# The inverse's identity written by GpSimd, sigmoids as tanh, and copies and scalings moved to ScalarE in the mixing stage of a hybrid decoder step

## The chip, the cores and the metric

The kernel runs on one core of a Trainium2 chip. A core has a matrix engine (TensorE, PE in the profile, its weight loads shown as PEld), VectorE (DVE), ScalarE (ACT), GpSimd (POOL) and SyncE (SP), which here only issues DMAs. The engines run side by side, each through a queue of its own in a fixed order, and wait for one another by semaphores. The metric is the time on the device of one execution, in microseconds (us).

## The reference

One layer of a decoder on 256 prompt tokens and 8 sampled tokens, all in fp32, with a width of 2048:

```python
x = x + 0.5 * swiglu(rmsnorm(x, n1), f1g, f1u, f1d)     # width 5504
proj = rmsnorm(x, nm) @ w_in
o_att  = sliding-window attention over q, k, v (16 heads of 64, window 128, sinks, relative bias)
o_rwkv = rwkv_time_mix(the other columns of proj)        # 16 heads of 64
x = x + concat(o_att, o_rwkv) @ w_out
x = x + 0.5 * swiglu(rmsnorm(x, n2), f2g, f2u, f2d)      # then a final rmsnorm
```

The part that the change touches is the second half of the mixing. The softmax of the attention is `exp(s - m) / denom`. The time mixing goes by these lines, where `a` is the rate and `g` the output gate:

```python
w = -softplus(-(w0 + tanh(wl) @ w2)) - 0.5;  logw = -exp(w)
a = sigmoid(a0 + al @ a2)
g = sigmoid(gl) @ g2
kk = k * k_k;  kk = kk / max(norm(kk), 1e-12)            # per head
k = k * (1.0 + (a - 1.0) * k_a)
S = S * exp(logw) + (S @ -kk) (kk * a)^T + v k^T;  y = S @ r   # token by token
```

## The kernel before

**Data and gemms.** The 264 tokens (256 + 8) are the free axis of every large product; the 2048 features lie in 16 tiles of 128 partitions. Each fp32 product is made of three products of a split, `hi*hi`, `hi*lo` and `lo*hi`. A weight block of four tiles (`chunk`, line 116) is loaded by SyncE's queue into a raw buffer, rounded to its high part by ScalarE (line 123), and the low part is the difference, on VectorE (the call on line 124, shown under line 58, the helper `tt`). Six raw buffers and four pairs of high and low parts go round. Twelve matmuls of 128x264 belong to one block (`gemm`, line 127).

**Stages.** First feed-forward, mixing (`mixing_body`, line 332), second feed-forward. In the mixing the input product is made tile by tile (`win`, line 365): two tiles for the low-rank inputs and the gate (lines 819 to 822), then three tiles for each of eight pairs of heads, then keys and values, then eight query tiles. Its result feeds small tasks, written as coroutines, which are moved on by one step after every weight block; `pause` puts a number of such steps between two parts of a task (`DWAIT`, `PW`). So the matmuls of a task stand among those of the gemms.

**The tasks.** `prep` (from line 392), one for each pair of heads: two small products give the decay and the rate, two sigmoids on ScalarE (lines 401, 402), the key's norm on VectorE (line 412), two exponentials of the running decay (lines 416 to 418), the rate's steps (lines 423 to 427), the decayed keys (`KR`, line 431), and copies of the eight sampled columns to `XD` by GpSimd (line 436). A pair's scores within a chunk of 64 tokens go to memory (`sa`).

`chain` (from line 516), one for each batch of two pairs, four batches: it inverts the unit triangular matrices of the delta rule. The 32x32 blocks are read back spread over partitions, as `X` and `Y` (shown as `Xt`; lines 528, 529); 30 steps of a substitution run on VectorE (lines 535 to 542). The result, which lacks the ones on its diagonal, is stored to memory (`sb`, line 544) by four transfers and read again into `TT` (line 549) in the layout of the matrix engine. VectorE then adds the identity to four blocks (lines 552 to 556), two transposes give `TN` (line 559), and products follow: TN's (line 566) copied to `zs` by ScalarE (571), `zs` with `TT` copied by ScalarE into `TT` (580), `TT` with `KR`. The last gives `W`, copied by ScalarE (594), and `uv`, copied by VectorE in two halves per pair (596). Then `PT` (610), `N` (626), three steps of the state, the output `y` (649) and a group norm (`gnorm`).

`softmax` (line 701) is called by each of eight `attend` tasks on four tiles, two of 128x256 and two of 128x128, and by `dec_attend` on one: four exponentials with their sums on ScalarE, a reciprocal and four scalings on VectorE. The maximum comes with the scores (`mxv`, line 732).

**Output product.** It goes in three passes over the heads (`PASS`): pairs 0 to 3 of the time mixing, pairs 4 to 7, and the attention. Ahead of each pass its inputs are split on ScalarE (line 858) and on VectorE and GpSimd in turn (line 859).

**Order.** The order of the program is made at build time by a list scheduler which knows the engines and estimates durations; the weight blocks have high priority and a few instructions are pinned. The code therefore gives the order only up to that scheduler: an edit of one task can move the instructions of others in all queues. Between the two programs here, the first 6566 and the last 6512 matrix instructions of 15622 stand in the same order; what differs lies in the mixing.

Of the kernel before, what the change touches and what calls it, by code (L numbers as in the profile page):

```python
# [9 lines left out]
AF = mybir.ActivationFunctionType  # L10
ALU = mybir.AluOpType
AX = mybir.AxisListType

P = 128
NP = 256
NB = 8
T = NP + NB
# [7 lines left out]
HALF = (slice(0, 64), slice(64, 128))  # L25
# [17 lines left out]
VMU, VKK, VKA, VA0, VRK, VLW, VLB, VSK, VSD = 64, 90, 98, 106, 114, 122, 130, 138, 154  # L43
# [4 lines left out]
def body(tc, I, O):  # L48
    nc = tc.nc
    V, A, G, TE, SP = nc.vector, nc.scalar, nc.gpsimd, nc.tensor, nc.sync  # L50
# [6 lines left out]
    def tt(e, out, a, b, op):  # L57
        return e.tensor_tensor(out=out, in0=a, in1=b, op=op)  # L58

    def stt(out, a, s, b, op0, op1):  # L60
        return V.scalar_tensor_tensor(out=out, in0=a, scalar=s, in1=b, op0=op0, op1=op1)  # L61

    def ts(e, out, a, s1, op0, s2=None, op1=None):
        k = {} if op1 is None else dict(op1=op1)
        e.tensor_scalar(out=out, in0=a, scalar1=s1, scalar2=s2, op0=op0, **k)

    def act(out, in_, f, **k):
        return A.activation(out=out, in_=in_, func=f, **k)  # L68

    def bc(ap, shape):  # L70
        return ap.broadcast_to(list(shape))
# [19 lines left out]
    def pause(n):  # L91
        for _ in range(n):
            yield

    with ExitStack() as ctx:
# [7 lines left out]
        def slot(shape=(P, T), dt=F32, tag="s"):  # L103
            return sp.tile(list(shape), dt, tag=tag, bufs={"s": NS, "o": NO, "y": NY}[tag], name=uid(tag))

        def tmp(shape=(P, T), dt=F32):
            pool, n = cur[0]
            return pool.tile(list(shape), dt, tag="t", bufs=n, name=uid("t"))
# [4 lines left out]
        def mp():  # L113
            return pp.tile([P, 512], F32, tag="m", bufs=NM, name=uid("m"))
# [28 lines left out]
        vec = cp.tile([P, NVEC], F32, name="vec")  # L143
# [13 lines left out]
        def vc(i):  # L157
            return vec[:, i:i + 1]
# [168 lines left out]
        def mixing(n2, n3, XD):  # L327
            with tc.tile_pool(name="mx", bufs=1) as mx:
                cur[0] = (mx, NT)
                return mixing_body(mx, n2, n3, XD)  # L330

        def mixing_body(mx, n2, n3, XD):
            def fix(shape, name):
                return mx.tile(list(shape), F32, name=name)

            def ring(shape, tag, bufs):
                return mx.tile(list(shape), F32, tag=tag, bufs=bufs, name=uid(tag))
# [6 lines left out]
            ident, bo, cm = C[:, CID:CID + P], C[:, CBO:CBO + P], C[:, CCM:CCM + P]  # L344
# [7 lines left out]
            for pj in PJ:  # L352
                G.memset(pj[:, 0:1], 0.0)
            nmu = fix((P, NSH), "nmu")
            mu = vec[:, VMU:VMU + NSH]
            ts(V, nmu, mu, -1.0, ALU.mult, 1.0, ALU.add)
            tt(V, ss, ss, bc(mu.unsqueeze(2), (P, NSH, NB)), ALU.mult)
# [15 lines left out]
            def shifted(t, d):  # L373
                ps = win(t)
                pj = PJ[t % 3]
                with tc.high_priority():
                    tt(V, pj[:, 1:1 + T], ps[:, :T], rs, ALU.mult)
                G.tensor_copy(shc[:, t, :], pj[:, NP:NP + NB + 1])
                act(d[:, :NP], pj[:, 0:NP], AF.Copy, scale=vc(VMU + t))
                A.copy(d[:, NP:], ss[:, t, :])  # L380
                stt(d, pj[:, 1:1 + T], nmu[:, t:t + 1], d, ALU.mult, ALU.add)
                return d

            la, sgl = fix((P, T), "la"), fix((P, T), "sgl")
# [4 lines left out]
            def c4(x):  # L389
                return x[:, :NP].rearrange("p (c t) -> p c t", c=4)  # L390

            def prep(p, bt, k, xrr, xk, xv):
                lw = load(I["lw"][p], (P, 256))
                zp = mp()
# [3 lines left out]
                ap = mp()  # L398
                mm(ap[:, :T], lw[:, P:2 * P], la)
                sg, a = tmp(), tmp()  # L400
                act(sg, zp[:, :T], AF.Sigmoid)
                act(a, ap[:, :T], AF.Sigmoid, bias=vc(VA0 + p))
                kk, b = tmp(), tmp()
                act(kk, xk, AF.Copy, scale=vc(VKK + p))
                act(b, kk, AF.Square)
# [8 lines left out]
                W, Wi = tmp((P, 4, 65)), tmp((P, 4, 64))  # L414
# [5 lines left out]
                yield from pause(PW[1])  # L420
                rk = tmp((P, T + 2 * NB))
                stt(b, b, 1e24, kk, ALU.min, ALU.mult)
                tt(V, b, b, a, ALU.mult)
                ts(V, a, a, 1.0, ALU.subtract, vc(VKA + p), ALU.mult)
                kx = a
                stt(kx, a, 1.0, xk, ALU.add, ALU.mult)
                stt(rk[:, :T], xrr, vc(VRK + p), kx, ALU.mult, ALU.mult)
                yield
                BK, KR = ring((P, 4, 3, 64), "bk", 2), ring((P, 3, 4, 64), "kr", NKR)
                bt.KR[k] = KR  # L430
                stt(KR[:, 0], c4(kk), -1.0, W[:, :, 0:64], ALU.mult, ALU.mult)
                tt(V, KR[:, 1], c4(xrr), W[:, :, 1:65], ALU.mult)
                s4 = (P, 4, 2, 64)
                tt(V, BK[:, :, 0:3:2, :], bc(c4(b).unsqueeze(2), s4), bc(Wi.unsqueeze(2), s4), ALU.mult)
                tt(V, BK[:, :, 1, :], c4(kx), Wi, ALU.mult)
                for i, src in ((6, kk), (2, b), (3, xv), (4, kx), (5, xrr)):
                    G.tensor_copy(XD[:, i, p, :], src[:, NP:T])
                dq = rk[:, T:].rearrange("p (s b) -> p s b", s=2)
                tt(G, XD[:, 7, p, :], XD[:, 1, p, :], XD[:, 5, p, :], ALU.mult)
# [31 lines left out]
                for h in range(2):  # L471
# [3 lines left out]
                    for blk in range(2):  # L475
                        x = blk * 32
# [39 lines left out]
            def chain(bt):  # L516
                n = bt.n
                while bt.left:
                    yield
                nr = n * 16  # L520
                ng = P // nr
                if ng == 3:
                    ng = 2
                nj = 32 // ng
                X = ring((ng * nr, 32, 32), "X", 1)
                Y = ring((ng * nr, nj, 32), "Xt", 1)
# [4 lines left out]
                TT = ring((P, n * 4, 64), "TT", NTT)  # L531
# [3 lines left out]
                for s in range(1, 31):  # L535
                    m, w = -(-s // ng), 31 - s
                    t = ring((ng * nr, m, w), "st", 2)
# [3 lines left out]
                    if s % NSTEP == 0:  # L541
                        yield
                for g in range(ng):
                    SP.dma_start(scr2[bt.i].rearrange("r (j g t) -> g r j t", g=ng, t=32)[g], Y[g * nr:(g + 1) * nr])  # L544
                yield from pause(1)
                for h in range(2):
                    for blk in range(2):
                        x = h * 64 + blk * 32
                        SP.dma_start(TT[x:x + 32, :, blk * 32:blk * 32 + 32],
                                     scr2[bt.i].rearrange("(h b m) (s t) -> h b s m t", h=2, b=2, s=32)[h, blk])  # L550
                yield from pause(DWAIT[bt.i])
                for h in range(2):
                    for blk in range(2):
                        x = h * 64 + blk * 32
                        v = TT[x:x + 32, :, blk * 32:blk * 32 + 32]
                        tt(V, v, v, bc(ident[x:x + 32, x:x + 32].unsqueeze(1), (32, n * 4, 32)), ALU.add)
                TN = ring((P, n * 4, 32), "TN", 1)
                for h in range(2):
                    V.transpose(TN[h * 64:h * 64 + 32], TT[h * 64:h * 64 + 32, :, 0:32])
# [2 lines left out]
                for k in range(n):  # L562
                    for c in range(4):
                        for h in range(2):
                            j = k * 4 + c
# [17 lines left out]
                uv = bt.UV  # L583
                W, PT = ring((P, n, 3, 64), "W", 1), ring((P, n, 3, 64), "PT", 1)
# [7 lines left out]
                for k in range(n):  # L592
                    v = wus[k].rearrange("p (c t) -> p c t", c=4)
                    A.copy(W[:, k], v[:, 1:4, 0:64])
                    for h in range(2):
                        V.tensor_copy(uv[HALF[h], :, k, HALF[h]], v[HALF[h], :, 64:128])
                yield
                pbs = [mp() for _ in range(n)]
                for k in range(n):
                    for c in range(1, 4):  # L600
                        x = (c - 1) * P
# [6 lines left out]
                for k in range(n):  # L608
                    v = pbs[k][:, :384].rearrange("p (c t) -> p c t", c=3)
# [3 lines left out]
                for k in range(n):  # L613
                    for c in range(4):
                        x = (k * 4 + c) * 64
# [3 lines left out]
                for k in range(n):  # L619
                    for c in range(4):  # L620
                        x = (k * 4 + c) * 64
# [8 lines left out]
                for c in range(1, 4):  # L630
# [5 lines left out]
                    for k in range(n):  # L636
                        for h in range(2):
                            r = HALF[h]
                            x = (k * 4 + c) * 64
# [20 lines left out]
                for k in range(n):  # L660
                    p, o = bt.p0 + k, Ys[k]
# [39 lines left out]
            def softmax(s, mxv, sinks, n):  # L701
                nm, sm, es = (ring((P, 4), "st" + x, 6) for x in "abc")
                ts(V, nm[:, :n], mxv[:, :n], -1.0, ALU.mult)
                for j in range(n):
                    act(s[j], s[j], AF.Exp, bias=nm[:, j:j + 1], accum_out=sm[:, j:j + 1])
                w = n // len(sinks)
                for h, x in enumerate(sinks):
                    act(es[:, h * w:(h + 1) * w], nm[:, h * w:(h + 1) * w], AF.Exp, bias=x)
                tt(V, sm[:, :n], sm[:, :n], es[:, :n], ALU.add)
                V.reciprocal(sm[:, :n], sm[:, :n])  # L710
                for j in range(n):
                    ts(V, s[j], s[j], sm[:, j:j + 1], ALU.mult)

            def attend(t, q):
                p = t // 4
# [12 lines left out]
                for h, sps in enumerate(spp):  # L728
                    s1, s0 = sc[h]
                    head = (2 * p + h) * 4 + t % 4  # L730
                    for s, a, b, j in ((s1, sps[:, 0:256], bs[h], 0), (s0, sps[:, 256:384], bs[h][:, P:256], 1)):
                        V.tensor_tensor_reduce(out=s, in0=a, in1=b, op0=ALU.add, op1=ALU.max, scale=1.0,  # L732
                                               scalar=vc(VSK + head), accum_out=mxv[:, 2 * h + j:2 * h + j + 1])
                softmax([x for y in sc for x in y], mxv, [vc(VSK + (2 * p + h) * 4 + t % 4) for h in range(2)], 4)
                yield
                yield from pause(PW[4])
# [82 lines left out]
            shifted(0, la)  # L819
            act(tw[0:64, :], la[0:64, :], AF.Tanh)  # L820
            shifted(1, sgl)
            act(sgl, sgl, AF.Sigmoid)
            bat, att, bts = [], [], []
            for kind, i in SEQ:
                if kind == "b":
                    bt = newbatch(i)
                    for k in range(BATCH[i]):
                        p = bt.p0 + k
                        x = [shifted(2 + 3 * p + j, tmp()) for j in range(3)]
# [5 lines left out]
                elif kind == "kv":  # L835
                    w, p = i // 2, i % 2
                    ps = win(LKV + i)
                    x = slot()
# [86 lines left out]
        with tc.tile_pool(name="dx", bufs=1) as dx:  # L925
            XD = dx.tile([P, 8, NPAIR, NB], F32, name="XD")
# [101 lines left out]
```

## Time and profile before

| | |
|---|---|
| time, median of 3 runs | 2034.14 us (2033.25 to 2035.09) |
| the profiled execution | 2030.2 us |
| its span in the trace | 2028.1 us |
| mean granted TensorE clock | 0.996 |
| busy: PE, DVE, ACT, POOL | 98%, 65%, 51%, 12% |

The profiled execution took 2.1 us more than its span, which runs from the first to the last instruction that the trace shows. Rows of a view name the line of the kernel, the engine, the operation and its output and inputs (`TT<-TT,C` reads the tiles TT and C and writes TT); behind the bar stand the busy time, the mean duration of one in ns, and the idle time of the engine just before such instructions with what ended it. `A <- B: 5.3, 5, 1.5` in the views of waits reads: A waited for B, 5.3 us in total, 5 times, 1.5 at the longest. In a timeline, a row starts with its start and its duration; a value in square brackets is the idle time of the engine before it. A granted clock of 1.00 is TensorE's full rate.

### The profile page before, as it was taken

The numbers are of one execution on the slowest core, as the hardware profiler recorded it, in microseconds if no ns is written. First come the engines' busy times: TensorE is split into PE (matmuls) and PEld (weight loads), VectorE is DVE, ScalarE is ACT, GpSimd is POOL, SyncE is SP. The second block draws the span as 40 slices with busy tenths as digits, with TensorE's granted clock in tenths as the row PEclk, the third lists the DMA queues.
The fourth block names the chain that finished last, engine by engine and source line by source line (L and its number), as shares of the span: only waits on it lengthen the run. The fifth ranks groups of instructions, "written<-read, shape, count | busy, mean of one in ns | idle before, by whom it ended". The sixth has DMA issues, their size and how long they took to land.

```text
span 2028.1 us, 45390 instructions
## 1 busy us (share of the span) xinstructions
PE 1994.5 (98%) x17096; PEld 1956.8 (96%) x17096; DVE 1321.9 (65%) x2623; ACT 1035.2 (51%) x2027; POOL 240.9 (12%) x337
## 2 busy tenths in 40 slices
PE   9999999999999999999999899999999999999998
PEld 9999999999999999998898789999999999999998
DVE  5865555655556577678778766775666666666665
ACT  5644444444444466665555455554444444444445
POOL 0301001010110122111100010120101101010012
PEclk9999999999999999999999899999999999999999
DMA  6565655655556566554455345465566555655654
GB/s 226 178 187 196 184 193 188 185 185 176 186 170 192 181 207 204 155 159 121 134 148 166 91 133 185 171 184 178 191 181 195 180 192 189 187 191 180 195 181 145
DMA packets 227421, 358.38 MB, mean 177 GB/s; under 512 B 42353, under 2 KB 80769, under 8 KB 227201
## 3 DMA queue, kind: packets, MB, share of 16 engines
q1 hardware_dynamic: 220752, 346.95, 55.0%
q10 hardware_dynamic: 6448, 8.53, 1.3%
q8 instruction: 134, 2.20, 0.5%
q14 instruction: 87, 0.70, 0.1%
HBM read 347.25 MB, written 10.21 MB: 176 GB/s over the span
## 4 chain that ended last, share of the span: by engine, by line
PE 93%; DVE 3%; DMA 2%; ACT 1%; issue 1%; SPq 0%; ACTq 0%; DVEq 0%
PE acc L74 84%; PE m L74 7%; DVE lo L58 1%; DMA TT<-sb 1%; DMA sb<-Xt 0%; DMA raw<-in_win 0%; DVE y L58 0%; ACT t L68 0%; DVE t L678 0%; DMA raw<-in_gu 0%; DVE Xt L58 0%; DVE st L58 0%; ACT L68 0%; SPq L544 0%; DVE t L732 0%
## 5 line engine op out<-in xcount | busy, mean ns | idle before, releaser
L58 DVE TENSOR_TENSOR lo<-raw,hi 128x512 fp32r<-128x512 f32 (+1 forms) x1288 | 869.3, 679 | 546.4 <-ACT hi L123 518.5
L123 ACT CAST hi<-raw 128x512 fp32r<-128x512 f32 (+1 forms) x1288 | 775.9, 607 | 860.2 <-PE acc L74 777.6
L74 PE MATMUL acc<-s,hi 128*128 128x264 f32 x5940 | 1107.3, 286 | 4.7 <-ACT hi L123 2.5
L74 PEld LDWEIGHTS acc<-s,hi 128*128 128x128 f32 x5940 | 921.9, 188 | 10.3 <-issue 4.0
L74 PE MATMUL acc<-s,lo 128*128 128x264 f32 x2970 | 848.1, 286 | 5.3 <-DVE lo L58 5.3
L74 PEld LDWEIGHTS acc<-s,lo 128*128 128x128 f32 x2970 | 558.9, 188 | 8.8 <-DVE lo L58 6.6
L74 PE MATMUL acc<-t,hi 128*128 128x264 f32 x2752 | 503.0, 284 | 0.0
L74 PEld LDWEIGHTS acc<-t,hi 128*128 128x128 f32 x2752 | 426.3, 188 | 0.0
L74 PE MATMUL acc<-t,lo 128*128 128x264 f32 x1376 | 388.9, 285 | 0.0
L58 POOL TENSOR_TENSOR t<-t,t 128x264 f32<-128x264 f32 (+1 forms) x148 | 150.7, 1018 | 1151.2 <-ACT hi L123 791.0
L74 PEld LDWEIGHTS acc<-t,lo 128*128 128x128 f32 x1376 | 258.4, 188 | 0.1
L74 PE MATMUL acc<-y,hi 128*128 128x264 f32 x648 | 124.5, 284 | 0.0
L74 PEld LDWEIGHTS acc<-y,hi 128*128 128x128 f32 x648 | 101.8, 189 | 0.2
L74 PE MATMUL acc<-y,lo 128*128 128x264 f32 x324 | 92.5, 285 | 0.0
L58 DVE TENSOR_TENSOR t<-acc,t 128x264 f32<-128x264 f32 x156 | 67.4, 432 | 37.1 <-PE acc L74 36.9
L74 PE MATMUL acc<-o,hi 128*128 128x264 f32 x324 | 63.5, 286 | 0.0
L58 POOL TENSOR_TENSOR o<-o,o 128x264 f32<-128x264 f32 x43 | 35.9, 834 | 230.8 <-ACT o L68 225.1
L74 PEld LDWEIGHTS acc<-y,lo 128*128 128x128 f32 x324 | 60.8, 188 | 0.0
L61 DVE SCALAR_TENSOR_TENSOR s<-acc,s 128x264 f32<-128x264 f32 x96 | 40.6, 427 | 16.0 <-PE acc L74 15.5
L74 PEld LDWEIGHTS acc<-o,hi 128*128 128x128 f32 x324 | 50.3, 188 | 0.0
L74 PE MATMUL m<-s,hi 128*128 128x264 f32 x260 | 48.5, 285 | 0.0
L61 DVE SCALAR_TENSOR_TENSOR x<-acc,x 128x264 f32<-128x264 f32 x96 | 40.5, 427 | 10.0 <-PE acc L74 9.6
(236 smaller groups left out, 1288.7 us busy)
## 6 DMA issues: line engine op xcount, KB each, us to landing
raw<-in_gu SPq DMA_DIRECT2D x688, 256.0 KB, 3.3
raw<-in_dn SPq DMA_DIRECT2D x224, 256.0 KB, 2.8
raw<-in_win SPq DMA_DIRECT2D x152, 256.0 KB, 3.4
raw<-in_dn SPq DMA_DIRECT2D x160, 192.0 KB, 2.7
raw<-in_wout SPq DMA_DIRECT2D x64, 256.0 KB, 3.2
xsp<-x ACTq DMA_DIRECT2D x16, 132.0 KB, 3.2
s<-xsp SPq DMA_DIRECT2D x16, 132.0 KB, 4.2
ld<-in_sT SPq DMA_DIRECT2D x16, 128.0 KB, 3.2
```

What stands on the lines that cost most here:

```text
L58: return e.tensor_tensor(out=out, in0=a, in1=b, op=op)
L61: return V.scalar_tensor_tensor(out=out, in0=a, scalar=s, in1=b, op0=op0, op1=op1)
L74: TE.matmul(out, lhsT, rhs, start=start, stop=stop, **k)
L123: A.copy(hi[:, :w], raw[:, :w])
```

## The change

All edits are in the mixing stage.

- The sigmoids become `0.5 * tanh(0.5 x) + 0.5`. For the decay and the gate the affine part is a GpSimd step of 128x264 (nine in all). The rate `a` stays a plain tanh: `kk * a` becomes `(a + 1) * kk` with the factor one half put into `KR` (-0.5 in place of -1) and into the sampled column 6 of `XD`, which GpSimd now scales while it copies. Two small tiles, `half` and `less`, hold half of the key's rate weight, half of the rate's bias, and one minus the former.
- The rate's affine step `1 + (a - 1) k_a` moves from VectorE to one ScalarE pass per pair, and the product with the key is a plain multiplication.
- The identity: behind the substitution GpSimd writes 1.0 to the diagonal of `Y` with a strided memset for each of four groups of partitions, ahead of the store to `sb`. The store waits for these. The four additions per batch behind the return trip are dropped.
- Of the two `uv` copies per pair, the second goes to ScalarE.
- Of the four softmax scalings, the last two (the second head's) go to ScalarE.

```diff
+            half = fix((P, 16), "half")
+            ts(V, half, vec[:, VKA:VKA + 16], 0.5, ALU.mult)
+            less = fix((P, 8), "less")
+            ts(V, less, half[:, 0:8], -1.0, ALU.mult, 1.0, ALU.add)
...
-                act(sg, zp[:, :T], AF.Sigmoid)
-                act(a, ap[:, :T], AF.Sigmoid, bias=vc(VA0 + p))
+                act(sg, zp[:, :T], AF.Tanh, scale=0.5)
+                ts(G, sg, sg, 0.5, ALU.mult, 0.5, ALU.add)
+                act(a, ap[:, :T], AF.Tanh, scale=0.5, bias=half[:, 8 + p:9 + p])
...
-                tt(V, b, b, a, ALU.mult)
-                ts(V, a, a, 1.0, ALU.subtract, vc(VKA + p), ALU.mult)
+                stt(b, a, 1.0, b, ALU.add, ALU.mult)
+                act(a, a, AF.Identity, scale=half[:, p:p + 1], bias=less[:, p:p + 1])
                 kx = a
-                stt(kx, a, 1.0, xk, ALU.add, ALU.mult)
+                tt(V, kx, a, xk, ALU.mult)
...
-                stt(KR[:, 0], c4(kk), -1.0, W[:, :, 0:64], ALU.mult, ALU.mult)
+                stt(KR[:, 0], c4(kk), -0.5, W[:, :, 0:64], ALU.mult, ALU.mult)
...
-                for i, src in ((6, kk), (2, b), (3, xv), (4, kx), (5, xrr)):
+                ts(G, XD[:, 6, p, :], kk[:, NP:T], 0.5, ALU.mult)
+                for i, src in ((2, b), (3, xv), (4, kx), (5, xrr)):
...
                 for g in range(ng):
+                    G.memset(Y[g * nr:(g + 1) * nr].rearrange("p j t -> p (j t)")[:, g:g + (nj - 1) * (32 + ng) + 1:32 + ng], 1.0)
+                for g in range(ng):
                     SP.dma_start(scr2[bt.i].rearrange("r (j g t) -> g r j t", g=ng, t=32)[g], Y[g * nr:(g + 1) * nr])
...
-                for h in range(2):
-                    for blk in range(2):
-                        x = h * 64 + blk * 32
-                        v = TT[x:x + 32, :, blk * 32:blk * 32 + 32]
-                        tt(V, v, v, bc(ident[x:x + 32, x:x + 32].unsqueeze(1), (32, n * 4, 32)), ALU.add)
...
-                        V.tensor_copy(uv[HALF[h], :, k, HALF[h]], v[HALF[h], :, 64:128])
+                        (V.tensor_copy, A.copy)[h](uv[HALF[h], :, k, HALF[h]], v[HALF[h], :, 64:128])
...
-                    ts(V, s[j], s[j], sm[:, j:j + 1], ALU.mult)
+                    if j < 2:
+                        ts(V, s[j], s[j], sm[:, j:j + 1], ALU.mult)
+                    else:
+                        act(s[j], s[j], AF.Copy, scale=sm[:, j:j + 1])
...
-            act(sgl, sgl, AF.Sigmoid)
+            act(sgl, sgl, AF.Tanh, scale=0.5)
+            ts(G, sgl, sgl, 0.5, ALU.mult, 0.5, ALU.add)
```

## The prediction

> **What bounds the kernel now.** I read the page's head and its chain first, then busy time by stretch, then the waits of the one stretch that has any.
>
> ```profile
> span 2028.1 us, 45390 instructions
> ...
> PE 1994.5 (98%) x17096; PEld 1956.8 (96%) x17096; DVE 1321.9 (65%) x2623; ACT 1035.2 (51%) x2027; POOL 240.9 (12%) x337
> ...
> PE 93%; DVE 3%; DMA 2%; ACT 1%; issue 1%; SPq 0%; ACTq 0%; DVEq 0%
> ```
>
> The matrix engine (PE) is busy 98% of the span and carries 93% of the chain that ended last. No other engine is over 65%. Work taken off VectorE (DVE) or ScalarE (ACT) is worth nothing where PE has matmuls to run; it pays only where PE stands idle or its clock drops. The next view says where that is. Its columns are the stretch in us, then busy time and instructions of PE, PEld, DVE, ACT and POOL, then the granted PE clock, the DMA share and GB/s.
>
> ```profile
> 770.00:890.00 120.00, 119.96 (x1102) 115.69 (x1102) 92.64 (x220) 82.40 (x185) 24.03 (x61) 1.00 0.57 169
> 890.00:1099.00 209.00, 197.19 (x2201) 183.23 (x2199) 160.47 (x454) 113.14 (x261) 20.88 (x57) 1.00 0.50 140
> 1099.00:1180.00 81.00, 72.60 (x653) 59.12 (x653) 60.96 (x209) 42.32 (x129) 4.48 (x10) 0.94 0.40 117
> 1180.00:1212.00 32.00, 32.00 (x258) 28.65 (x256) 19.75 (x58) 15.28 (x42) 3.94 (x12) 1.00 0.50 148
> 1212.00:2016.00 804.00, 804.00 (x6595) 802.89 (x6594) 516.64 (x892) 399.10 (x716) 90.16 (x96) 1.00 0.58 182
> ```
>
> The mixing stage runs from about 770 to 1212 us. PE is idle 209.00 - 197.19 = 11.8 us in its middle and 81.00 - 72.60 = 8.4 us in its tail, 20.2 us in all, and the tail's clock of 0.94 loses about 0.06 x 81 = 4.9 us more. The second feed-forward has no idle time at all, and its code isn't touched. So the change can win 25 us at the very most (1.2%), and in practice only the part of it that it shortens. The waits of PE between 890 and 1180 us (total, times, longest):
>
> ```profile
> PE acc L74 <- DVE lo L58: 5.3, 5, 1.5
> PE m L74 <- DVE uv L596: 3.8, 5, 1.9
> PE m L74 <- DVE mxv L732: 3.1, 2, 2.3
> PE acc L74 <- DVE s L58: 2.1, 1, 2.1
> PE m L74 <- ACT y L649: 1.4, 1, 1.4
> ...
> PE m L74 <- DVE TN L559: 0.6, 1, 0.6
> ```
>
> Here "lo" is the low half of a weight chunk, "s" an input slot or split, "uv", "TN", "W", "y" the delta rule's pieces, "mxv" the softmax maximum. What makes "lo" and "s" late is one thing, seen in VectorE's own waits and in the timeline of batch 3:
>
> ```profile
> DVE TT L58 <- DMA TT<-sb: 13.2, 4, 4.3
> ```
>
> ```profile
> 1106.00 0.17 DVE L58 TENSOR_TENSOR Xt<-Xt,st 128x8 f32<-128x8 f32 x1
> ...
> 1114.61 0.41 DVE L58 TENSOR_TENSOR TT<-TT,C 32x256 f32<-32x256 f32 x1 [2.42 <-DMA TT<-sb]
> ```
>
> ```profile
> 1115.51 0.48 PE L74 MATMUL acc<-s,hi 128*128 128x264 f32 x2 [2.10 <-DVE s L58]
> ```
>
> The last substitution step ends at 1106.17; the inverse goes to memory and back, and VectorE stands still for it until 1114.61. Everything queued behind on VectorE, weight splits included, stands too, and PE runs dry for 2.10 us. Four batches, 13.2 us of such standing.
>
> **The change part by part.** What leaves and joins each engine, by these rows (count, total, mean ns):
>
> ```profile
> L596 DVE COPY uv<-m 64x256 f32<-64x256 f32 x16 | 6.7, 420 | 0.3
> L58 DVE TENSOR_TENSOR TT<-TT,C 32x256 f32<-32x256 f32 x16 | 6.7, 417 | 13.6 <-DMA TT<-sb 13.2
> L65 DVE TENSOR_SCALAR t<-t,stb 128x256 f32<-128x256 f32 x16 | 5.6, 349 | 0.1
> ...
> L65 DVE TENSOR_SCALAR t<-t,stb 128x128 f32<-128x128 f32 x16 | 4.5, 279 | 0.0
> ...
> L65 DVE TENSOR_SCALAR t<-t,vec 128x264 f32<-128x264 f32 x8 | 2.8, 352 | 0.0
> ```
>
> ```profile
> L68 ACT ACT_TABLE_LOAD x24 | 30.8, 1283 | 4.6 <-PE m L74 4.2
> ...
> L68 ACT ACTIVATE t<-t,sta 128x256 f32<-128x256 f32 x16 | 8.0, 501 | 8.0 <-DVE sta L65 7.9
> L68 ACT ACTIVATE t<-t,sta 128x128 f32<-128x128 f32 x16 | 6.2, 387 | 0.0
> ...
> L501 ACT COPY BT<-m 64x256 f32<-64x256 f32 x16 | 5.9, 366 | 0.2
> ...
> L68 ACT ACTIVATE t<-t,vec 128x264 f32<-128x264 f32 x8 | 4.1, 514 | 0.0
> ...
> L594 ACT COPY W<-m 128x192 f32<-128x192 f32 x8 | 2.5, 319 | 4.3 <-PE m L74 4.2
> ```
>
> VectorE loses 16 identity additions (6.7 us), 8 of 16 value copies (8 x 0.42 = 3.4), the rate's affine step (2.8) and half of the softmax scalings (8 x (0.349 + 0.279) = 5.0): 17.9 us. ScalarE gains the copies (8 x 0.366 = 2.9), the affine (8 x 0.514 = 4.1) and the scalings (8 x (0.501 + 0.387) = 7.1, by its own passes of those shapes), 14.1 us. It loses table loads: in the two programs as built, 14 of them are gone, because the sigmoids have become tanh and share a table with the exponentials, 14 x 1.283 = 18.0 us. Net ScalarE -3.9. All of this lies under busy PE; as totals it is worth nothing. What follows is what it does at the idle places.
>
> GpSimd (POOL) gains 9 affine steps, 8 scalings of the sample columns in place of copies, and 16 sets of ones, 4 a batch.
>
> ```profile
> L58 POOL TENSOR_TENSOR s<-o,s 128x264 fp32r<-128x264 f32 x4 | 3.4, 879 | 1.2 <-ACT s L858 1.2
> ...
> L533 POOL MEMSET TT<- 32x256 f32 x8 | 2.4, 306 | 5.4 <-PE m L74 5.1
> ```
>
> *Sigmoid path.* Between the decay's sigmoid and its exponential stood a table load (1.28); now a GpSimd step stands there, between VectorE's 0.35 and the 0.88 of a GpSimd pass of that size, and a hop between engines. From +0.3 to -0.6 us for each pair, under weight gemms that kept PE at 119.96 of 120.00 us in the stretch where most of it lies: 0. Were that cover gone, 8 x 0.3 = 2.4 at worst.
>
> *Identity.* The four additions of 0.42 after the return trip go. In their place four GpSimd memsets stand between the last substitution step and the store, at most 0.31 each and one of them early, so +0.5 us (0.3 to 1.5 with the hop) on a trip of 8.44. VectorE's standing does not go away: its transposes read the same transferred tile and are the next to wait, for about 13 us again. Queued behind them are the weight splits "lo"; before, some of these had to let additions pass too. Per batch that is +0.5 for the hop and -0.8 for two additions ahead of the split that PE wants. In batches 0 to 2, where the "lo" and "TN" rows come to 5.3 + 0.6 us (0.6 of the 5.3 in the tail), I take -1; bounds 3 x 1.5 = +4.5 and -5.3.
>
> *Value copies.* A batch had W, W on ScalarE (2 x 0.32 = 0.64) and four copies on VectorE (1.68) before the next matmuls. Now it is W, uv, W, uv on ScalarE: 0.32 + 0.37 + 0.32 + 0.37 = 1.38, and two copies on VectorE, 0.84. The end comes 0.3 earlier where both engines are free (1.2 for four batches), more where VectorE was behind (1.90 once), while the second W comes 0.37 later (+1.5 at worst). I take -1.5; bounds +1.5 and -3.8, the whole uv row.
>
> *Tail.* This is the largest term, and its sign is open. As built, the change reorders it. Before, batch 3's matmuls on the transposed inverse stand 86 matmuls into the first output pass; in the changed program they stand right behind the last input gemm, ahead of that pass. PE then has nothing else while that chain goes step by step, and on ScalarE the steps stand behind exponentials that themselves wait for VectorE:
>
> ```profile
> 1104.17 0.51 ACT L68 ACTIVATE t<-t,sta 128x256 f32<-128x256 f32 x1 [3.54 <-DVE sta L65]
> ...
> 1105.94 0.47 ACT L68 ACTIVATE stc<-sta,vec 128x2 f32<-128x2 f32 x2
> 1106.31 0.40 ACT L858 CAST s<-y 128x264 fp32r<-128x264 f32 x1
> ```
>
> One softmax holds ScalarE 2.14 us. Walking the built queues with the rows' durations from the end of the second transpose: PE has waited 0.9 to 2.4 us for it; one softmax and two copies later (2.14 + 0.73) it gets the next operand, idle 2.5; the following product is through at +6.9; the first input split of the output pass stands behind more softmaxes with their moved scalings and comes at +9.1, idle 2.3, then smaller waits of 0.7, 0.2, 0.75 and 0.6. Together 8 to 9.5 us idle. A clock loss comes on top, because of these rows:
>
> ```profile
> 1116.00:1118.00 2.00, 1.41 (x8) 1.41 (x9) 1.94 (x6) 0.00 (x0) 0.00 (x0) 0.75 0.11 35
> 1118.00:1120.00 2.00, 2.00 (x10) 1.70 (x10) 1.94 (x4) 0.62 (x1) 0.00 (x0) 0.50 0.78 212
> ...
> 1159.00:1161.00 2.00, 2.00 (x7) 1.64 (x8) 2.00 (x9) 0.15 (x1) 0.00 (x0) 0.50 0.33 88
> 1161.00:1163.00 2.00, 2.00 (x7) 0.85 (x7) 1.10 (x4) 1.97 (x4) 0.00 (x0) 0.50 0.32 109
> ```
>
> After the idle 2.10 us the clock was 0.75 and then 0.50 for some 4 us, and again around 1160. I add 2 us for it and 1 to 1.5 for later waits (later in the tail the changed order mixes gemm and small matmuls more evenly): 11 to 12.5, against 8.2 + 4.9 = 13.1 now. I take -1; bounds -8 (the chain finds cover after all) and +8 (each of the three long waits a softmax, 2.14, longer, and the clock halved for the few us behind).
>
> The Trainium skill, TensorE: Matmul & The Clock Gate, the practical table at its end, allows idle gaps of up to about 3 µs before the clock falls. The rows of 1116 to 1120 disagree: 2.10 us sufficed. By that rule the new gaps of 2.3 to 2.5 us would cost no clock, and the sum would be some 2 us lower.
>
> **Sum.** -1 -1.5 -1 = -3.5 us: 2030.2 - 3.5 = 2026.7 for the profiled execution. The runs' median is 2034.14, 3.9 above it, so 2030.6 for the median.
>
> **The rivals.** *Faster (2025).* The tail's own waits go: "mxv" 3.1, "s" 2.1 and the half clock around 1160 (about 3 us) are VectorE being late, and VectorE is what is relieved. That is -8, with 1 to 2 for uv. For it: VectorE is busy 60.96 of 81 there, ScalarE only 42.32. Against: the new order puts a chain in the open that gemms covered.
>
> *Slower (2041).* ScalarE's queue after the last input gemm. If zs, the splits and W each wait one softmax longer than I walked, that is 3 x 2.14 = 6.4 us, plus 2 for the clock, less 1.5: +7. It decides from 1.2 us per step upward (3 x 1.2 = 3.6 takes the gain away). For it: 7.1 us of scalings join that queue. Against: ScalarE has 38.7 us free there.
>
> *Contention (2034).* Two rows on VectorE bear on GpSimd's new work:
>
> ```profile
> L58 DVE TENSOR_TENSOR s<-o,s 128x264 fp32r<-128x264 f32 x4 | 3.1, 792 | 0.6 <-ACT s L858 0.6
> ...
> L58 DVE TENSOR_TENSOR s<-y,s 128x264 fp32r<-128x264 f32 x4 | 1.6, 426 | 0.0
> ```
>
> The same subtraction takes 792 ns or 426, and the slow four run while GpSimd does the like. Nine new steps at 0.37 are 3.3 us of VectorE, mostly covered; if a third batch's splits are hit, the gain is gone. The Trainium skill, GPSIMD Engine Reference, section Specifications, has GpSimd share its SBUF interfaces with VectorE and names instructions with two SBUF inputs; the two rows agree.
>
> That the change doesn't do what it says is half true already: the standing of 13.2 us stays, as reckoned above.
>
> **How the numbers follow.** About 0.2%, 4 us, is what a measurement of this kernel tells from no change. The small gain has 0.45 (2026 to 2036 by itself, 0.18 of it faster by over 0.2%, 0.27 same), the faster rival 0.20, the slower one 0.27 (0.04 of it same), contention 0.08 (half same, half slower). Faster 0.38, same 0.35, slower 0.27. The range 2022 to 2042 leaves out the far ends of both rivals.
>
> **What would show it.** Right: 14 table loads fewer; no additions of the identity; VectorE's wait for the return trip moved to the transposes at 11 to 15 us; PE's "uv" wait under 2.5; idle time of 2 us and more right behind the last input gemm; PE's idle sum of the stage at 15 to 20. Wrong: new idle time outside 890 to 1180, "hi" or "s" of ScalarE heading PE's waits, or a clock under 0.90 in the tail.

## The result and the profile after

The changed kernel takes 2018.14 us (median of 4 runs, 2015.66 to 2019.98), the kernel before 2034.62 beside it (2033.25 to 2035.76): a ratio of 0.9907 with an interval of 0.9885 to 0.9929. In a later series it was 2016.32 against 2033.21, 0.9917 (0.9897 to 0.9937). By the medians it is faster by 16 to 17 us; -3.5 had been forecast, with a range from 2022 us up.

The page's head and its chain, changed kernel:

```profile
span 2016.2 us, 45438 instructions
...
PE 1993.4 (99%) x17096; PEld 1960.2 (97%) x17096; DVE 1307.2 (65%) x2577; ACT 1032.4 (51%) x2045; POOL 255.3 (13%) x362
...
PE 94%; DMA 2%; DVE 2%; ACT 1%; issue 1%; SPq 0%; DVEq 0%; ACTq 0%; POOL 0%; POOLq 0%
```

The profiled executions are 2030.2 and 2017.98 us, 12.2 apart; the other 4 us stand between the medians only, since the profiled execution of before is among its fastest. The span is 11.9 shorter, and PE's idle time in it fell from 2028.1 - 1994.5 = 33.6 to 22.8, by 10.8. Busy time by stretch, the kernel before and then the changed one (columns as above):

```profile
890.00:1060.00 170.00, 159.53 (x1734) 149.15 (x1732) 131.51 (x359) 94.11 (x217) 18.70 (x53) 1.00 0.49 137
1060.00:1215.00 155.00, 145.26 (x1400) 124.62 (x1399) 111.74 (x362) 78.56 (x217) 11.17 (x25) 0.97 0.45 131
```

```profile
890.00:1060.00 170.00, 165.50 (x1840) 154.91 (x1840) 124.11 (x343) 94.27 (x227) 28.05 (x69) 0.99 0.53 142
1060.00:1215.00 155.00, 149.40 (x1387) 133.02 (x1384) 113.12 (x353) 88.11 (x238) 12.23 (x28) 0.94 0.48 138
```

Idle time is 10.5 before and 4.5 after in the first stretch, 9.7 and 5.6 in the second. VectorE has 7 us less to do in the first stretch, ScalarE 10 us more in the second; both stay under 80%. The clock fell from 0.97 to 0.94 in the tail, so the gain comes in spite of it. The waits of PE in the mixing, changed kernel:

```profile
PE m L74 <- DMA ld<-in_bias: 2.3, 1, 2.3
PE m L74 <- DVE TN L562: 2.1, 2, 1.1
PE m L74 <- DMA ld<-in_cv: 1.6, 1, 1.6
PE acc L74 <- DVE lo L58: 1.4, 1, 1.4
PE m L74 <- ACT W L597: 1.4, 2, 0.7
PE m L74 <- ACT uv L599: 0.4, 1, 0.4
PE acc L74 <- DVE s L58: 0.2, 1, 0.2
```

"uv" on VectorE (3.8), "mxv" (3.1), "y" (1.4), "N" (1.2) and both "t" are gone, "lo" fell from 5.3 to 1.4 and "s" from 2.1 to 0.2. TN rose from 0.6 to 2.1 (both waits are batch 0's), W from 0.5 to 1.4, and two waits on loads are new. By the times, the first of these is a wait for `zs`: ScalarE writes it from 1097.23 on, behind a softmax, and PE goes on at 1097.64.

```profile
1097.23 0.75 ACT L574 COPY zs<-m 32x256 f32<-32x256 f32 x2
```

VectorE still stands for the return trip, at the transposes now:

```profile
DVE TN L562 <- DMA TT<-sb: 11.5, 6, 3.5
```

What changed most is when batch 3's chain runs, and what stands beside it:

```profile
1083.83 0.18 DVE L58 TENSOR_TENSOR Xt<-Xt,st 128x8 f32<-128x8 f32 x1
...
1092.77 0.43 DVE L562 STREAM_TRANSPOSE TN<-TT 32x256 f32<-32x256 f32 x1 [1.35 <-DMA TT<-sb]
1094.21 0.43 DVE L562 STREAM_TRANSPOSE TN<-TT 32x256 f32<-32x256 f32 x1
```

Its substitution ends at 1084.0 us, not 1106.2. The effect is far behind that place. The next rows count only the gemm matmuls (those into "acc"), in the same ten microseconds of the kernel before and of the changed one:

```profile
1150.00:1160.00 10.00, 0.00 (x0) 0.00 (x0) 0.00 (x0) 0.00 (x0) 0.90 0.05 16
```

```profile
1150.00:1160.00 10.00, 6.09 (x44) 5.27 (x42) 1.27 (x3) 0.00 (x0) 1.00 0.40 117
```

In the kernel before no gemm matmul runs at all there, and the DMAs move 16 GB/s. Its timeline shows the edges of that hole:

```profile
1147.73 0.29 PE L74 MATMUL acc<-s,lo 128*128 128x264 f32 x1
1149.37 1.16 PE L74 MATMUL m<-y,C 128*128 128x264 f32 x4 [1.36 <-ACT y L649]
...
1165.08 0.65 PE L74 MATMUL m<-t,s 128*64 128x256 f32 x4 [0.15 <-ACT t L742]
1165.65 0.51 PE L74 MATMUL acc<-s,hi 128*128 128x264 f32 x2
```

For 17.6 us, when the second output pass had only just begun (18 of its matmuls had run, by count), PE had only what batch 3's chain and the attention could give it: 12.8 us of small matmuls and 4.8 of idle time. The waits on y 1.36, t 0.90, mxv 2.26 and the half clock around 1160 all lie in this hole. The second pass can't go on until batch 3 has its outputs; its y is copied by 1149.6 us in the kernel before and by 1123.6 in the changed one, where the chain's substitution is 22 us earlier and the chain ends under the first pass.

The chain has not become free by that. In the changed kernel its first products stand between the last input gemm and the output pass, and a hole of 10.7 us (1093.6 to 1104.3) and one of 5.0 lie there; behind 1115 us the longest is 3.5. Counting the gemm matmuls in the two traces shows the trade. Behind 7700 of them the changed kernel is 5.1 us ahead of the kernel before; behind 7850, past its own two holes, 12.3 us late; behind 8000, past the old hole, 12.3 us ahead; behind 8200, at the end of the mixing, 10.8 ahead.

### The profile page after: what moved, and what is told of

The parts are those of the page before. It is cut to its first block, busy times and chain, and to the rows that moved or that the text cites. A ratio compares the mean times of both kernels' runs of the same rounds, so it can differ in the third digit from the quotient of the medians.

```text
span 2016.2 us, 45438 instructions
## 1 busy us (share of the span) xinstructions
PE 1993.4 (99%) x17096; PEld 1960.2 (97%) x17096; DVE 1307.2 (65%) x2577; ACT 1032.4 (51%) x2045; POOL 255.3 (13%) x362
## 4 chain that ended last, share of the span: by engine, by line
PE 94%; DMA 2%; DVE 2%; ACT 1%; issue 1%; SPq 0%; DVEq 0%; ACTq 0%; POOL 0%; POOLq 0%
PE acc L74 86%; PE m L74 8%; DVE lo L58 0%; ACT t L68 0%; DMA TT<-sb 0%; DVE y L58 0%; DMA sb<-Xt 0%; DMA raw<-in_win 0%; DMA ld<-in_cv 0%; DMA raw<-in_gu 0%; PE m L502 0%; DMA sa<-gm 0%; DMA out_vp<-s 0%; DVE st L58 0%; DVE Xt L58 0%
```

## The experiments

Sixteen runs were made, one of them the changed kernel again. Each median below has the kernel before at 2032 to 2035 in its own series; the ratio is to that. "Ends" is the end of batch 3's substitution and "holes" the stretches of over 8 us without a gemm matmul behind 1085 us, both read off the timeline; "idle" is the span less PE's busy time. These three are of the profiled execution.

| | median us | ratio (interval) | ends | holes us | idle us |
|---|---|---|---|---|---|
| before | 2034.62 | 1 | 1106.2 | 17.6 | 33.6 |
| changed | 2018.14 | 0.9907 (0.9885, 0.9929) | 1084.0 | 10.7 | 22.8 |
| identity alone | 2028.67 | 0.9976 (0.9964, 0.9987) | 1099.2 | 11.9 | 30.4 |
| tanh alone | 2029.02 | 0.9973 (0.9963, 0.9984) | 1106.2 | 10.1 | 30.6 |
| uv alone | 2031.94 | 0.9994 (0.9984, 1.0003) | 1102.3 | 15.2 | 32.4 |
| scalings alone | 2037.63 | 1.0014 (1.0001, 1.0027) | 1108.6 | 20.1 | 35.8 |
| identity and tanh | 2022.20 | 0.9942 (0.9925, 0.9958) | 1090.3 | 10.5 | 29.0 |
| changed, no identity | 2027.54 | 0.9969 (0.9957, 0.9980) | 1100.0 | 17.5 | 30.3 |
| changed, no tanh | 2024.14 | 0.9951 (0.9935, 0.9966) | 1102.7 | none | 26.7 |
| changed, no uv | 2022.31 | 0.9947 (0.9927, 0.9967) | 1090.0 | 10.7 | 27.4 |
| changed, no scalings | 2015.05 | 0.9907 (0.9891, 0.9923) | 1084.2 | 10.4 | 21.8 |
| changed, again | 2016.32 | 0.9917 (0.9897, 0.9937) | 1086.5 | 10.5 | 23.6 |
| later chain | 2037.47 | 1.0022 (1.0011, 1.0032) | 1086.9 | 15.9, 8.7, 11.0 | 32.6 |
| earlier chain | 2045.81 | 1.0056 (1.0039, 1.0073) | 1111.4 | 12.9, 10.7 | 43.0 |
| dummy additions | 2016.32 | 0.9923 (0.9908, 0.9938) | 1085.3 | 10.5 | 25.2 |
| rate on VectorE | 2029.06 | 0.9981 (0.9966, 0.9996) | 1096.7 | 13.4 | 29.6 |
| ones by VectorE | 2015.51 | 0.9918 (0.9901, 0.9934) | 1088.5 | 10.7 | 24.0 |
| pause of batch 1 | 2019.13 | 0.9940 (0.9925, 0.9955) | 1088.8 | 11.0 | 25.1 |

The times go with PE's idle time. The end of the substitution and the holes by themselves don't give their order: "no tanh" has no long hole and ends late, "no identity" has the old hole back and is still 7 us faster than the kernel before.

**Each part alone** in the kernel before. The edits are the change's own:

```diff
identity alone: the memsets of 1.0 in, the four additions out
tanh alone:     the Tanh, affine, KR, XD and half/less edits
uv alone:       (V.tensor_copy, A.copy)[h](uv...)
scalings alone: if j < 2: ts(V, ...) else: act(..., AF.Copy, scale=sm[:, j:j + 1])
```

> The kernel before with the identity part alone: GpSimd writes the ones into the spread inverse, VectorE's four additions per batch go. Theory M (each part wins the waits of TensorE that its own rows show): the waits on lo, s and TN, 8.0 us before and 3.7 in the changed kernel, fall to about 4, so -4 us (2030 by the median). Theory O (what counts is that any edit makes the scheduler order the mixing anew): the result is anywhere from -6 to +6 us and its waits by name do not fit the part.

> The kernel before with the tanh part alone (sigmoids as tanh, affine steps on GpSimd, the rate's step on ScalarE). Theory M: no wait of TensorE before had a sigmoid, a table load or the rate's step as its cause, so 0 to -1 us (2033 to 2034.6). Theory O: -6 to +6 us, with other waits gone than those of this part; 14 table loads fewer, which by themselves win nothing.

> The kernel before with half of the uv copies on ScalarE, nothing else. Theory M: the waits on uv and W, 4.3 us before and 1.8 in the changed kernel, fall to about 2, so -2.5 us (2032). Theory O: -6 to +6 us, not through these rows.

> The kernel before with half of the softmax scalings on ScalarE, nothing else. As built it differs from the kernel before only in the tail (the first 8557 matrix instructions stand in the same order). Theory M: the waits on mxv, y and t in the tail, 5.4 us, fall to 1 or less and the half clock around 1160 us goes, so -5 to -6 us (2029). Theory O: the tail's reordering gives -3 to +6 us, with new waits in place of the old.

The identity won 5 us, as its rows had it, but the rows don't fit: "lo" did fall, and a new wait stands at the end of the input gemms. It is named after "stb"; PE stands there in front of batch 3's matmuls on TN.

```profile
PE m L74 <- DVE stb L707: 8.0, 1, 8.0
PE acc L74 <- DVE lo L58: 3.1, 3, 1.6
PE m L74 <- DVE TN L556: 2.9, 2, 1.7
```

The tanh part, which touches no wait of PE, won as much. The uv part can't be told from nothing: its waits on uv went, and those on W rose from 0.5 to 5.6 us. The scalings, expected to win most, lost some 3 us, just clear of the noise. So theory M, each part by its own rows, fails in two of four, and theory O explains two.

**Each part undone** in the changed kernel, the same edits backwards:

```diff
no identity:  - G.memset(Y..., 1.0)            + four tt(V, v, v, ident..., ALU.add)
no tanh:      - AF.Tanh, ts(G, ...), AF.Identity   + AF.Sigmoid, tt(V, ...), ts(V, ...)
no uv:        - (V.tensor_copy, A.copy)[h]     + V.tensor_copy
no scalings:  - act(s[j], ..., AF.Copy, ...)   + ts(V, s[j], ...)
```

> The changed kernel with the identity part undone (VectorE's four additions per batch are back, no memsets). Alone that part gave 0.24%, 5 us. If the parts add, this comes 5 us above the changed kernel, 2023; if the parts need one another (the identity part alone ended in an 8.0 us wait on stb in the tail, which the changed kernel doesn't have), it gives back more, 2026 to 2030; if the order alone counts, it may land on either side of 2018.

> The changed kernel with the tanh part undone (sigmoids and 30 table loads are back, the rate's step on VectorE). Alone it gave 0.27%, 5.5 us. Adding parts: 2023.5. Parts that need one another: 2027 to 2030, with a long wait in the tail back. Order alone: either side of 2018.

> The changed kernel with both uv copies on VectorE again. Alone the part gave 1 us. Adding parts: 2019. By the uv rows (3.8 us before, 0.4 after): 2021. Order alone: either side of 2018 by some us.

> The changed kernel with all softmax scalings on VectorE again. Alone the part cost 3 us. Adding parts: 2015, faster than the changed kernel. If the scalings are what took the tail's waits on mxv away: 2021 to 2024, with mxv in the tail's waits again.

By the medians, against the changed kernel's 2018.14, the identity is worth 9.4, tanh 6.0, uv 4.2, and the scalings -3.1. So identity and uv are worth more in company than alone (5 and 1). No identity brings the hole of 17.5 us back. Without the scalings the kernel is no slower; that it beats the changed one isn't shown, the intervals lie on each other.

**Whether the place of batch 3's chain is the cause.** The first run is the changed kernel again. The other three:

```diff
identity and tanh: before + the identity edits + the tanh edits
later chain (changed kernel):   -DWAIT = (8,8,8,4)   +DWAIT = (8,8,8,16)
earlier chain (kernel before):  -DWAIT = (8,8,8,4)   +DWAIT = (8,6,6,2)
```

> The changed kernel itself, to stand beside the others of this series: 2016 to 2020. So far the time has followed one thing, the moment at which batch 3's substitution ends (1106.2 us in the kernel before, 1084.0 in the changed one; 1099 with the identity alone, 1102.7 without the tanh part, 1089.9 without the uv part). Theory C: that moment is the cause, the parts win by bringing batch 3's chain forward under the last input gemms. Theory W: the parts win each at its own waits, and the moment only goes along.

> The kernel before with the identity and the tanh part, without the uv copies and the scalings. Alone the two gave 5 and 5.5 us. As built, its substitution of batch 3 ends after 686 weight splits as in the changed kernel, not 692 as in the kernel before. Theory C: nearly the whole gain, 2016 to 2020, and an end at about 1088. Theory W: 5 + 5.5, so 2023.5 or more, with the uv waits of the kernel before (3.8 us) still there.

> The changed kernel with one number other: the last pause ahead of and behind batch 3's substitution is 16 weight blocks and not 4. All the work is the same. As built, the matmuls on TN of batch 3 stand after 7912 gemm matmuls (7776 in the changed kernel, 7874 in the kernel before); the substitution itself stands where it did on VectorE. Theory C: the gain of the tail is lost, +5 to +10 us (2023 to 2028), with waits on mxv, y or s in the tail. Theory W: within 2 us of the changed kernel.

> The kernel before with shorter pauses around the chains of batches 1 to 3 (6, 6, 2 weight blocks for 8, 8, 4), all work the same. As built, batch 3's matmuls on TN stand after 7776 gemm matmuls, as in the changed kernel, but its substitution still ends after 692 weight splits. If the place of the TN matmuls is what counts: about 2025 or less. If it is the end of the substitution on VectorE: no gain, 2031 to 2040, with PE waiting on TN or lo in front of the tail. Theory W: as the kernel before.

The later chain came to 2037.47, a ratio of 1.0022 (1.0011 to 1.0032): one number in a list of pauses, no work changed, and the whole gain of 17 us is gone with some more, which is more than theory C had forecast (2023 to 2028). Its substitution still ended at 1086.9; what moved is the chain behind it. Its waits in the mixing, and the gemm matmuls in two stretches:

```profile
PE acc L74 <- ACT s L865: 4.6, 1, 4.6
PE m L74 <- ACT t L748: 3.1, 1, 3.1
PE m L745 <- DVE t L65: 3.0, 1, 3.0
...
PE m L74 <- DVE y L61: 1.9, 1, 1.9
```

```profile
1160.00:1170.00 10.00, 1.39 (x3) 0.79 (x3) 0.00 (x0) 0.00 (x0) 0.51 0.01 1
1180.00:1190.00 10.00, 0.00 (x0) 0.00 (x0) 0.00 (x0) 0.00 (x0) 0.85 0.06 18
```

The holes are back, 15.9, 8.7 and 11.0 us long, and PE waits 4.6 for the splits "s" of the second pass, which wait for batch 3's y. The earlier chain in the kernel before took 2045.81, 1.0056 (1.0039 to 1.0073):

```profile
PE m L74 <- DVE TN L559: 16.2, 5, 10.5
```

There the matmuls on TN were ordered early, but the substitution ended at 1111.4, and PE stood 10.5 us in front of them at one time. Earlier alone is no gain, here it is a loss of 12 us: the substitution has to be done when PE arrives. Identity and tanh together gave 2022.20, about the sum of their single gains (5 + 5.5) and not the whole, nearer to theory W; the uv part on top (the row "no scalings") brings another 7, where alone it brought 1. So the parts add up in part only, and theory C in its strong form, that the moment decides everything, is wrong too. What is shown is that one pause, which moves this chain and leaves the work as it is, moves the time by 20 us, and that the changed kernel loses its whole gain when the chain stands late.

**What brings the chain forward.**

```diff
dummy additions (changed kernel):
+                for x in range(0, 128, 32):
+                    w = bc(ident[x:x + 32, x:x + 32].unsqueeze(1), (32, n * 4, 32))
+                    tt(V, TN[x:x + 32], w, w, ALU.add)
rate on VectorE (changed kernel, no scalings):
-                act(a, a, AF.Identity, scale=half[:, p:p + 1], bias=less[:, p:p + 1])
+                ts(V, a, a, half[:, p:p + 1], ALU.mult, less[:, p:p + 1], ALU.add)
ones by VectorE (changed kernel, no scalings):
-                    G.memset(Y[g * nr:...], 1.0)
+                    V.memset(Y[g * nr:...], 1.0)
pause of batch 1 (changed kernel, no scalings):
-DWAIT = (8,8,8,4)
+DWAIT = (8,7,8,4)
```

> The changed kernel with sixteen additions of 32x256 more on VectorE, in the number and size of the dropped identity additions, writing the tile TN ahead of its transposes; they depend on no transfer, and the built order of batch 3's chain stays as in the changed kernel. Theory L (the identity part wins because VectorE has 6.7 us less to do): back up by 3 to 9 us, 2020 to 2026. Theory C (it wins because the chain is ordered earlier): 2016 to 2019, as the changed kernel.

> The changed kernel without the scalings and with the rate's affine step on VectorE instead of ScalarE; so of the tanh part only the table loads and GpSimd's affine steps are left. Without the scalings alone it is 2015.05. As built, batch 3's substitution ends after 687 to 689 weight splits (687 there), TN stands after 7776 gemm matmuls. If the tanh part's 5 to 6 us come from VectorE's 2.8 us: 2019 to 2021. If they come from ScalarE's table loads: 2015 to 2017.

> The changed kernel without the scalings and with the ones written by VectorE, four memsets a batch, so that the store waits for no second engine. If GpSimd's hop ahead of the store costs: 0.3 to 1 us per batch less, 2011 to 2014. If not: 2015. If GpSimd's work beside VectorE was costly it would show here too.

> The changed kernel without the scalings and with batch 1's pause 7 weight blocks in place of 8. As built, batches 1 and 2 come 12 to 23 gemm matmuls earlier and batch 3's TN stays after 7776. Theory C, by which earlier isn't better in itself once the chain has cover: 2013 to 2018. It would be faster than both kernels if the lo waits of batches 1 and 2 (1.7 us) went.

Dummy additions: 2016.32, 0.9923 (0.9908 to 0.9938), the changed kernel's time with VectorE's 6.7 us back. But the sixteen ran well ahead of their transposes: batch 3's at 1051 to 1053 us, where the dropped ones stood at 1114.6 to 1119.5 in the kernel before. So 6.7 us of VectorE under gemms are worth nothing. What the additions cost in their old place, between the return trip and the transposes, was not tested; the identity part won either by that place or by the order in which the program was built. Ones by VectorE: 2015.51, 0.9918 (0.9901 to 0.9934), so GpSimd's hop ahead of the store costs nothing that can be measured. The pause of batch 1: 2019.13, 0.9940 (0.9925 to 0.9955), no better. The rate on VectorE was the surprise: 2029.06, 0.9981 (0.9966 to 0.9996), 14 us lost by an operation of 0.35 us per pair. Neither forecast made for it (by VectorE's 2.8 us, by the table loads) comes near; its waits show where the time goes:

```profile
PE m L74 <- DVE stb L58: 6.1, 1, 6.1
PE m L74 <- ACT W L597: 3.8, 3, 2.4
PE m L74 <- DVE TN L562: 3.5, 2, 2.6
```

The table loads are gone in it as well, batch 2's substitution ends at 1024.9 as in the changed kernel, but batch 3's ends at 1096.7 in place of 1084.2. PE comes to TN's matmuls at the end of the input gemms and stands 6.1 us (the row named "stb") and 2.6 us. Why the scheduler ordered it so wasn't followed; that a neutral-looking edit moves it by 12 us is what the run shows.

## Why the prediction was wrong, point by point

**What bounds the kernel: right.** All but about 1 us of the gain lies in the mixing, and 10.8 of the span's 11.9 us are PE's idle time.

**The totals: right in kind.** 14 table loads went (10 rows left in the mixing of 24); VectorE lost 14.7 us by the page, 17.9 forecast, ScalarE 2.8 (3.9). These totals are worth nothing by themselves, as said; the dummy additions show it for VectorE's time under gemms.

```profile
L68 ACT ACT_TABLE_LOAD x10 | 12.8, 1283 | 0.5 <-PE m L74 0.3
L68 ACT ACTIVATE t<-t,less,half 128x264 f32<-128x264 f32 x8 | 4.9, 610 | 11.8 <-DVE t L61 11.6
```

The rate's pass took 610 ns on ScalarE where 514 was taken; GpSimd's affine step took 497, inside the bounds of 0.35 and 0.88 us.

**Sigmoid path, 0: wrong in the outcome.** The path itself has no wait in either kernel, but the part is worth 5.5 to 6 us; as no row of its own shows them, the order is what is left.

**Identity, -1, and value copies, -1.5: wrong in size.** That the standing of 13.2 us stays was right (11.5), though for batch 3 VectorE stood only for the last 2.42 of the 8.44 us between 1106.17 and 1114.61, as its row says, and worked before. "lo" fell by 3.9, where -1 was taken in all for it and TN. The identity is worth 5 alone and 9.4 in company.

The copies alone won 1 us, with an interval that takes in zero, and 4.2 in company; the uv row went from 3.8 to 0.4, and W from 0.5 to 1.4. Together the two terms stand for the middle of the stage, from 6000 to 7700 gemm matmuls, and there the changed kernel won 5.6 us, not 2.5.

**Tail, -1: this is the step that failed most.** From 7700 to 8200 gemm matmuls the kernel before takes 131.2 us and the changed one 125.5, so the tail won 5.7 (a second profile of the changed kernel has 9.0, and 4.1 for the middle). The walk began from the end of the second transpose and laid the built order of PE and ScalarE on it; when the substitution would end, it did not say. (By the trace the matmuls on TN stood 98 gemm matmuls into the first pass before, not 86.) One link of it held: behind TN PE waited 2.5 us by the walk and 2.26 in the trace for zs, and a softmax of ScalarE stood in front of it, as reckoned.

```profile
1092.84 0.61 PE L74 MATMUL m<-sgl,ld 128*128 128x264 f32 x2
1093.09 0.48 PE L74 MATMUL acc<-s,lo 128*128 128x264 f32 x1
1093.50 0.93 PE L74 MATMUL m<-s,o 64*128 64x256 f32 x8
1094.36 1.03 PE L74 MATMUL m<-TN,gm 32*32 32x32 f32 x32
1097.64 0.31 PE L74 MATMUL m<-TT,zs 32*32 32x32 f32 x2 [2.26 <-DMA ld<-in_bias]
```

But TN, reckoned 0.9 to 2.4 us late, came as PE arrived: the substitution ended 22 us sooner, and score matmuls stood ahead of TN's. The splits of the first pass, reckoned at 2.3 and four smaller waits, were there in time. So PE idled 2.4 us between the last input gemm and the output pass, and 3.1 up to 1142 us, where 8 to 9.5 had been summed. (With clock and later waits 11 to 12.5 were given; the parts come to 13 at the upper end.) The second failure is on the other side: the old tail's 13.1 us were counted as waits and clock, not as a hole of 17.6 us that closes when the chain is done before the second pass needs it. The rival "faster" named the right rows (mxv, s, the half clock) and gave them to a relieved VectorE. The later chain speaks against that as the whole cause: it keeps all of VectorE's relief and loses all of the gain. The dummy additions don't bear on it, since none of them ran in the tail.

**Scalings: right in sign for the slower rival, small in size.** They cost some 3 us alone, and about as much or nothing in the changed kernel. **Contention: a real price, on fewer operations than before.** The four subtractions with the mean of 792 ns were three of 779 to 986, each beside GpSimd's like one, and one of 434 without. After, one of the four ran beside GpSimd's subtraction, at 977 ns; the others took 426 to 433, a mean of 567.

**The clock.** It fell from 0.996 to 0.992 over the span, which would be some 8 us if all matmuls took the loss in full. They didn't: counted from start to start without the idle time, the 14,496 gemm matmuls took 1788.3 us before and 1789.4 after, the 2600 others 205.9 and 203.7. One of the half-clock stretches, 1097.6 to 1104.4, lies in the hole, where no gemm matmul ran. So pricing the clock by the length of a stretch, as the tail's sum did, can go wrong by several us.

**Left open.** It is not known why the scheduler brings the chain forward with the parts that it does, nor what of the 16 us belongs to the chain's place and what to the single waits that went; no run separates the two in the changed kernel.

## What to carry to other kernels

Where a scheduler makes the order, compare the end of each long chain in the two built programs before adding up durations; one number in a list of pauses, which moved one chain, was worth 20 us here. A pass that needs the output of such a chain leaves a hole if the pass before it runs out first: look for stretches without gemm matmuls, not only for waits, because small matmuls hide such a hole as busy time. And test a gain of freed time by putting the time back without its wait, and look where it lands: the dummy additions here landed somewhere else.

## What was not expected of the hardware

The clock also fell without any idle time. In the changed kernel PE worked through a row of 24 matmuls of 8 columns, and the rows behind it read half clock at full busy time:

```profile
1166.01 2.74 PE L74 MATMUL m<-t,ld 128*128 128x8 f32 x24
```

```profile
1168.00:1172.00 4.00, 4.00 (x26) 4.00 (x26) 2.46 (x9) 2.09 (x6) 0.00 (x0) 0.66 0.74 224
1172.00:1176.00 4.00, 4.00 (x19) 4.00 (x20) 0.88 (x3) 0.89 (x2) 0.00 (x0) 0.50 0.48 125
```

The kernel before ran the same 24 at 1200.53 and kept 1.00 behind them, so it doesn't always happen. A wait of 2.26 us at 1095.4 to 1097.6 was followed by a clock of 0.50 up to 1104.4, like the 2.10 of the kernel before. The length of a wait doesn't decide it alone: 1.90 us at 914.3 in the kernel before and 2.48 us at 1064.5 in the second profile of the changed kernel cost no clock. The Trainium skill, TensorE: Matmul & The Clock Gate, in its practical table, asks for no idle gaps above about 3 µs; the two gaps that cost clock were shorter, and the measurement decides.
